# One weight difference from the DMA queue to VectorE, a quadrant fetched one step earlier, and a final norm by whole rows on VectorE

## The chip, the cores and the metric

The kernel runs on one core of a Trainium2 chip. A core has five engines with a queue each: TensorE (PE in the profile, with its weight loads as PEld), VectorE (DVE), ScalarE (ACT), GpSimd (POOL) and SyncE (SP). Each takes its own instructions in order and meets the others through semaphores. DMA transfers are issued from the queues of SP, ACT and POOL. The metric is device time in microseconds (us) of one execution; lower is better.

## The reference, cut to what matters

One layer of an encoder on 1024 positions of width 1024, in float32. The change touches the end of it, the down projection of the gated MLP and the last layer norm:

```python
def conv_ffn(x, w_up, conv_w, conv_b, w_down):
    h = depthwise_conv(x @ w_up, conv_w, conv_b)
    g, v = jnp.split(h, 2, axis=-1)
    return (jax.nn.silu(g) * v) @ w_down          # (1024 x 2816) @ (2816 x 1024)

h = layer_norm(DEEPNORM_ALPHA * h + ffn, ln_ffn_g[i], ln_ffn_b[i])
```

with `layer_norm(x) = (x - mean) * rsqrt(var + 1e-5) * g + b` over the 1024 columns of a row.

## The kernel before, in words

Every float32 product is made of three matmuls (`mm3`, L185, L187, L189): both operands are split into a rounded high part and the rest (`split`: a cast on ScalarE, L179, and a subtraction on VectorE, L176), and high times high, high times low and low times high are summed in PSUM.

The down projection is a block scheme of **seven products instead of eight**. The gated activations lie in DRAM (`gd`) as four quadrants `g(k, h)`, k the half of the inner dimension and h the half of the rows; the weights `wd` likewise as `w(k, h)`, h the half of the output columns. Product s = 0 to 6 multiplies a sum or difference of activation quadrants, `xa`, by one of weight quadrants, `xb`. Each product runs over six blocks b of the inner dimension (two slices of 128 each, the last one slice); a block is 24 matmuls in groups of three (12 in the last), so products 0 to 5 have 132 matmuls each. Product 6 runs row by row of the output, so that rows can be finished one after the other.

For every (s, b) three steps are recorded ahead of the matmuls: `down_load` fetches quadrants on SP's queue, `down_pile` adds to them, and `down_prep` splits `xa` into `ga` and `xb` into `wb`. Addition is done by the DMA itself: `pile` (L1095) is a DMA on POOL's queue that accumulates onto its destination. A subtraction is a `negate` on ScalarE (L1098), then a pile. Two tiles per block live long: `sst[b]` (named `sa`) is the running sum of activations, `tst[b]` (`sb`) that of weights. Product 3 needs xa = g(1,1) + sst and xb = tst - w(0,0); both start from a fresh fetch (`qa`, `qw`).

The order on PE, VectorE, ScalarE and POOL is the order in which the code records it (a manual schedule). At step n of the list of (s, b), `down_prep` is done up to two blocks ahead, `down_pile` and `down_load` some blocks more. `extra` adds the work between products: loading the residual (`acc`), adding a finished product's four PSUM banks to it (`down_out`, L1310), and residual scaling (L1178, L1179).

The end: after product 5, `last_row` takes rows 4 to 7 and then, as product 6 gives each, rows 0 to 3. It forms mean and variance (L1334, L217), the inverse deviation by a power on POOL (L218), and calls `finish`. There a row's first columns are done by two VectorE instructions and its last 512 (192 in row 3) by ScalarE and two POOL instructions (L1279, L1280); then SP sends the row out. Row 3, the last of all, goes out in three pieces.

Of the kernel before, what the change touches and what calls it, by code (L numbers as in the profile page):

```python
# [10 lines left out]
F32 = mybir.dt.float32  # L11
F32R = mybir.dt.float32r
AF = mybir.ActivationFunctionType
ALU = mybir.AluOpType
# [133 lines left out]
def encoder_layer(ctx: ExitStack, tc: tile.TileContext, a, out: bass.AP):  # L148
# [940 lines left out]
    def fetch(name, src, b):  # L1089
        t = t4([P, 2, 512], F32, name)  # L1090
        nc.sync.dma_start(out=t[:, 0 : span(b)], in_=src)
        return t
# [9 lines left out]
    def quads_of(b):  # L1102
# [5 lines left out]

        return g, w

    def down_load(s, b):
        g, w = quads_of(b)
        if s == 0:
            tst[b] = fetch(f"sb{b}", w(0, 0), b)
            dsrc[s, b] = fetch(f"qa{s}{b}", g(0, 0), b), tst[b]
        elif s == 1:
            sst[b] = fetch(f"sa{b}", g(0, 1), b)
            dsrc[s, b] = sst[b], tst[b]
        elif s == 2:
            dsrc[s, b] = sst[b], tst[b]  # L1120
        elif s == 3:
            dsrc[s, b] = fetch(f"qa{s}{b}", g(1, 1), b), fetch(f"qw{s}{b}", w(0, 0), b)
        elif s == 4:
            dsrc[s, b] = sst[b], fetch(f"qw{s}{b}", w(1, 1), b)
        elif s == 5:
            dsrc[s, b] = fetch(f"qa{s}{b}", g(1, 1), b), tst[b]
        else:
            dsrc[s, b] = fetch(f"qa{s}{b}", g(1, 0), b), fetch(f"qw{s}{b}", w(1, 0), b)

    def down_pile(s, b):  # L1130
        g, w = quads_of(b)
        n = span(b)
        xa, xb = dsrc[s, b]
        if s == 1:
            negate(xb, b)
            pile(xa, g(1, 1))
            pile(xb, w(0, 1))
        elif s == 2:
            negate(xa, b)
            negate(xb, b)  # L1140
            pile(xa, g(0, 0))
            pile(xb, w(1, 1))
        elif s == 3:
            negate(xb, b)
            pile(xa, sst[b][:, 0:n])
            pile(xb, tst[b][:, 0:n])
        elif s == 4:
            pile(xa, g(1, 0))
        elif s == 5:
            negate(xb, b)  # L1150
            pile(xb, w(1, 0))

    def down_prep(s, b):
        n = span(b)
        xa, xb = dsrc.pop((s, b))
        g = [t4([P, 2, 2, 256], F32R, f"ga{s}{b}{l}") for l in range(2)]
        w = [t4([P, 2, 512], F32R, f"wb{s}{b}{l}") for l in range(2)]
        split(g[0][:, 0:n], g[1][:, 0:n], xa[:, 0:n].rearrange("p k (j u) -> p k u j", u=2))
        hi, lo = [x[:, 0:n] for x in w]
        if s == 2:  # L1160
            nc.scalar.mul(hi, xb[:, 0:n], -1.0)
            nc.vector.scalar_tensor_tensor(
                out=lo, in0=xb[:, 0:n], scalar=-1.0, in1=raw(hi), op0=ALU.mult, op1=ALU.subtract
            )
        else:
            split(hi, lo, xb[:, 0:n])
        dops[s, b] = g, w
# [91 lines left out]
    def finish(i):  # L1259
        mv, rs = fin.pop(i)  # L1260
        rc = slice(i * P, (i + 1) * P)
        z = acc[i]
        n = 512 if i != 3 else 832
        c, d = slice(0, n), slice(n, 1024)
        nb = st([P, 1], F32, f"nb{i}")
        nc.vector.scalar_tensor_tensor(
            out=z[:, c], in0=z[:, c], scalar=mv[:, 0, 0:1], in1=ffg[:, c], op0=ALU.subtract, op1=ALU.mult
        )
        nc.vector.scalar_tensor_tensor(  # L1269
            out=nb, in0=mv[:, 0, 0:1], scalar=-1.0, in1=rs, op0=ALU.mult, op1=ALU.mult  # L1270
        )
        nc.scalar.activation(out=z[:, d], in_=z[:, d], func=AF.Identity, scale=rs, bias=nb)  # L1272
        for e in (c,) if i != 3 else (slice(0, 448), slice(448, n)):
            nc.vector.scalar_tensor_tensor(
                out=z[:, e], in0=z[:, e], scalar=rs, in1=ffb[:, e], op0=ALU.mult, op1=ALU.add
            )
            if i == 3:
                nc.sync.dma_start(out=out[rc, e], in_=z[:, e])
        nc.gpsimd.tensor_tensor(out=z[:, d], in0=z[:, d], in1=ffg[:, d], op=ALU.mult)  # L1279
        nc.gpsimd.tensor_tensor(out=z[:, d], in0=z[:, d], in1=ffb[:, d], op=ALU.add)  # L1280
        if i != 3:
            nc.sync.dma_start(out=out[rc], in_=z)
        else:
            nc.sync.dma_start(out=out[rc, d], in_=z[:, d])

    order = [(s, b) for s in range(7) for b in range(NB)]
    banks = {}
# [86 lines left out]
    for n, (s, b) in enumerate(order[: 6 * NB]):  # L1374
        if s < 2 and b == 0:
            banks[s] = [bank(f"dn{s}{rb}") for rb in range(4)]
        for step, lead in ((down_load, 3), (down_pile, 2), (down_prep, 0)):
            while done[step] < min(len(order), reach(n) + lead):
                step(*order[done[step]])
                done[step] += 1  # L1380
        down_mm(s, b, range(4), banks[s % 2], slice(0, 512), s < 2 and b == 0, b == NB - 1)
        extra(s, b)
        if (s, b) == (4, 0):
            ffg, ffb = row(5, "ffg"), row(6, "ffb")
# [36 lines left out]
```

## Time and profile before

| | |
|---|---|
| median of 3 runs | 880.27 us (879.35 to 881.75) |
| profiled execution | 879.64 us, of which the span from first to last instruction is 877.9 us |
| mean granted TensorE clock | 0.97 of full speed |
| TensorE busy | 813.2 us, 93% of the span |
| VectorE busy | 721.1 us, 82% |
| ScalarE, GpSimd busy | 401.8 us and 424.6 us |

The span is one profiled execution. Busy shares are means over stages with different limits, so a stage is read by itself: the rows below give stretches by their time from the start of the span. The down projection's products run from about 635 us on, the norm of the last rows from about 835 us. A row of the timeline gives the start, the duration, the engine, the line of the code, the operation and its tiles, and in brackets the idle time ahead of it with what ended it.

### The profile page before, as it was taken

The numbers are of one execution on the slowest core, as the hardware profiler recorded it, in microseconds if no ns is written. First come the engines' busy times: TensorE is split into PE (matmuls) and PEld (weight loads), VectorE is DVE, ScalarE is ACT, GpSimd is POOL, SyncE is SP. The second block draws the span as 40 slices with busy tenths as digits, with TensorE's granted clock in tenths as the row PEclk, the third lists the DMA queues.
The fourth block names the chain that finished last, engine by engine and source line by source line (L and its number), as shares of the span: only waits on it lengthen the run. The fifth ranks groups of instructions, "written<-read, shape, count | busy, mean of one in ns | idle before, by whom it ended". The sixth has DMA issues, their size and how long they took to land. (4 is left out here: it accounts for less than half of the span.)

```text
span 877.9 us, 10479 instructions
## 1 busy us (share of the span) xinstructions
PE 813.2 (93%) x3803; PEld 668.5 (76%) x3803; DVE 721.1 (82%) x980; ACT 401.8 (46%) x602; POOL 424.6 (48%) x274
## 2 busy tenths in 40 slices
PE   8984989967799999999999999999999999899992
PEld 6884967857688788888888888888878877688882
DVE  5999698999988898888888878888696865668856
ACT  4524381563354434444343444343564734466311
POOL 4579498878824455333455543334043322311075
PEclk9997999989899999999999999999999999999997
DMA  9305531131112223322222233222899999999212
GB/s 354 118 1 149 158 144 49 49 120 62 59 49 96 73 72 97 109 83 72 73 72 72 75 107 106 73 72 72 290 357 216 232 277 238 257 287 313 84 79 114
DMA packets 37492, 118.13 MB, mean 135 GB/s; under 512 B 4216, under 2 KB 5112, under 8 KB 37440
## 3 DMA queue, kind: packets, MB, share of 16 engines
q1 hardware_dynamic: 23408, 80.61, 26.2%
q0 software_dynamic: 7696, 25.31, 14.3%
q10 hardware_dynamic: 6336, 11.54, 3.5%
q8 instruction: 30, 0.49, 0.2%
q14 instruction: 22, 0.18, 0.1%
HBM read 91.75 MB, written 19.92 MB: 127 GB/s over the span
## 5 line engine op out<-in xcount | busy, mean ns | idle before, releaser
L1081 POOL TENSOR_TENSOR t<-t,t 128x1024 f32<-128x1024 f32 x22 | 54.6, 2482 | 241.3 <-DVE t L1046 177.1
L1046 DVE SCALAR_TENSOR_TENSOR t<-c,cols,t 128x1 f32<-128x1 f32 (+2 forms) x264 | 141.9, 585 | 3.7 <-ACT t L1071 0.5
L185 PE MATMUL by<-b,a 128*128 128x512 f32 (+1 forms) x268 | 106.2, 396 | 3.7 <-DVE c L922 3.7
L187 PE MATMUL dn<-wb,ga 128*128 128x512 f32 x264 | 105.2, 398 | 4.0 <-DVE wb L176 2.4
L185 PE MATMUL dn<-wb,ga 128*128 128x512 f32 x264 | 105.0, 398 | 3.7 <-DVE ga L176 2.3
L189 PE MATMUL by<-b,a 128*128 128x512 f32 (+1 forms) x268 | 105.6, 394 | 0.0
L187 PE MATMUL by<-b,a 128*128 128x512 f32 (+1 forms) x268 | 105.5, 394 | 0.0
L189 PE MATMUL dn<-wb,ga 128*128 128x512 f32 x264 | 104.5, 396 | 0.0
L176 DVE TENSOR_TENSOR a<-s,a 128x512 fp32r<-128x512 f32 x85 | 88.7, 1043 | 14.9 <-ACT a L873 14.6
L185 PE MATMUL bz<-b,a 128*128 128x512 f32 (+1 forms) x180 | 71.4, 397 | 3.5 <-DVE a L176 3.5
L187 PE MATMUL bz<-b,a 128*128 128x512 f32 (+1 forms) x180 | 71.3, 396 | 3.0 <-DVE b L176 3.0
L185 PE MATMUL bx<-b,a 128*128 128x512 f32 (+1 forms) x192 | 72.2, 376 | 1.2 <-ACT c L989 1.2
L176 DVE TENSOR_TENSOR a<-wr,a 128x512 fp32r<-128x512 f32 x64 | 71.5, 1120 | 1.9 <-ACT a L873 1.9
L187 PE MATMUL bx<-b,a 128*128 128x512 f32 (+1 forms) x192 | 71.9, 375 | 0.0
L189 PE MATMUL bx<-b,a 128*128 128x512 f32 (+1 forms) x192 | 71.9, 374 | 0.0
L189 PE MATMUL bz<-b,a 128*128 128x512 f32 (+1 forms) x180 | 71.1, 395 | 0.0
L185 PEld LDWEIGHTS by<-b,a 128*128 128x128 f32 x268 | 51.3, 191 | 16.1 <-DVE c L922 4.9
L187 PEld LDWEIGHTS dn<-wb,ga 128*128 128x128 f32 x264 | 49.9, 189 | 17.8 <-DVE wb L176 4.2
L185 PEld LDWEIGHTS dn<-wb,ga 128*128 128x128 f32 x264 | 50.0, 189 | 16.3 <-ACT wb L179 2.7
L922 DVE TENSOR_TENSOR c<-bz,c 128x512 f32<-128x512 f32 x44 | 30.4, 691 | 38.8 <-PE bz L189 38.0
L1230 ACT COPY c<-bx 128x512 f32<-128x512 f32 x22 | 12.9, 587 | 104.7 <-DVE c L922 104.7
L189 PEld LDWEIGHTS by<-b,a 128*128 128x128 f32 x268 | 51.2, 191 | 11.6
(340 smaller groups left out, 2005.5 us busy)
## 6 DMA issues: line engine op xcount, KB each, us to landing
wr<-wup SPq DMA_DIRECT2D x44, 512.0 KB, 4.5
gd<-t ACTq DMA_DIRECT2D x44, 256.0 KB
qa<-gd SPq DMA_DIRECT2D x20, 512.0 KB, 6.0
sa<-gd POOLq DMA_DIRECT2D x15, 512.0 KB, 15.7
sb<-wd POOLq DMA_DIRECT2D x15, 512.0 KB, 12.2
qw<-wd SPq DMA_DIRECT2D x15, 512.0 KB, 10.1
winT<-winT SPq DMA_DIRECT2D x8, 512.0 KB, 7.3
x<-x SPq DMA_DIRECT2D x8, 512.0 KB, 10.7
```

What stands on the lines that cost most here:

```text
L176: eng.tensor_tensor(out=lo, in0=src, in1=raw(hi), op=ALU.subtract)
L185: nc.tensor.matmul(outs[i], ll, rh[i], start=first, stop=False, **kw)
L187: nc.tensor.matmul(outs[i], lh, rl[i], start=False, stop=False, **kw)
L189: nc.tensor.matmul(outs[i], lh, rh[i], start=False, stop=last, **kw)
L922: nc.vector.tensor_tensor(out=o, in0=b, in1=x, op=ALU.add)
L1046: nc.vector.scalar_tensor_tensor(out=t[:, lo:hi], in0=c[:, lo + sh : hi + sh], scalar=w[:, wi : wi + 1], in1=t[:, lo:hi], op0=ALU.mult, op ...
L1081: nc.gpsimd.tensor_tensor(out=tg, in0=tg, in1=tv, op=ALU.mult)
L1230: nc.scalar.copy(out=cg[:, 0:512], in_=bx[j])
```

## The change

Three edits. In product 3 the weight difference is no longer a `negate` on ScalarE and an accumulating DMA, but one subtraction on VectorE at the head of `down_prep`. The fetch of `sst[b]` is recorded in product 0 (`early`) instead of in product 1's `down_load`. In `finish` a row is two VectorE instructions over all 1024 columns; only row 3 gives 224 columns of its second step to ScalarE and POOL, and ACT's queue sends that piece.

```diff
+    def early(b):
+        sst[b] = fetch(f"sa{b}", quads_of(b)[0](0, 1), b)
+
     def down_load(s, b):
...
         elif s == 1:
-            sst[b] = fetch(f"sa{b}", g(0, 1), b)
             dsrc[s, b] = sst[b], tst[b]
...
         elif s == 3:
-            negate(xb, b)
             pile(xa, sst[b][:, 0:n])
-            pile(xb, tst[b][:, 0:n])
...
     def down_prep(s, b):
         n = span(b)
         xa, xb = dsrc.pop((s, b))
+        if s == 3:
+            nc.vector.tensor_tensor(out=xb[:, 0:n], in0=tst[b][:, 0:n], in1=xb[:, 0:n], op=ALU.subtract)
...
         z = acc[i]
-        n = 512 if i != 3 else 832
-        c, d = slice(0, n), slice(n, 1024)
-        nb = st([P, 1], F32, f"nb{i}")
         nc.vector.scalar_tensor_tensor(
-            out=z[:, c], in0=z[:, c], scalar=mv[:, 0, 0:1], in1=ffg[:, c], op0=ALU.subtract, op1=ALU.mult
+            out=z, in0=z, scalar=mv[:, 0, 0:1], in1=ffg, op0=ALU.subtract, op1=ALU.mult
         )
-        nc.vector.scalar_tensor_tensor(
-            out=nb, in0=mv[:, 0, 0:1], scalar=-1.0, in1=rs, op0=ALU.mult, op1=ALU.mult
-        )
-        nc.scalar.activation(out=z[:, d], in_=z[:, d], func=AF.Identity, scale=rs, bias=nb)
-        for e in (c,) if i != 3 else (slice(0, 448), slice(448, n)):
+        pieces = (slice(0, 1024),) if i != 3 else (slice(0, 400), slice(400, 800))
+        if i == 3:
+            d = slice(800, 1024)
+            nc.scalar.activation(out=z[:, d], in_=z[:, d], func=AF.Identity, scale=rs)
+            nc.gpsimd.tensor_tensor(out=z[:, d], in0=z[:, d], in1=ffb[:, d], op=ALU.add)
+        for e in pieces:
             nc.vector.scalar_tensor_tensor(
                 out=z[:, e], in0=z[:, e], scalar=rs, in1=ffb[:, e], op0=ALU.mult, op1=ALU.add
             )
...
-        nc.gpsimd.tensor_tensor(out=z[:, d], in0=z[:, d], in1=ffg[:, d], op=ALU.mult)
-        nc.gpsimd.tensor_tensor(out=z[:, d], in0=z[:, d], in1=ffb[:, d], op=ALU.add)
...
+            nc.sync.dma_start(out=out[rc, e], in_=z[:, e])
+        if i == 3:
+            nc.scalar.dma_start(out=out[rc, d], in_=z[:, d])
...
+        if s == 0:
+            early(b)
         down_mm(s, b, range(4), banks[s % 2], slice(0, 512), s < 2 and b == 0, b == NB - 1)
```

POOL's queue, from product 3's piles on (`qa` is xa, `qw` is xb), before:

```order
L1095 DMA qa_5752<-sa_5290 128x1024
L1095 DMA qw_5754<-sb_4985 128x1024
L1095 DMA qa_5794<-sa_5334 128x1024
L1095 DMA qw_5796<-sb_5110 128x1024
L1095 DMA qa_5835<-sa_5375 128x1024
L1095 DMA qw_5837<-sb_5114 128x1024
```

and now, with the first pile of product 4 (`sa<-gd`) as the last row:

```order
L1095 DMA qa_5752<-sa_5248 128x1024
L1095 DMA qa_5794<-sa_5300 128x1024
L1095 DMA qa_5833<-sa_5347 128x1024
L1095 DMA qa_5872<-sa_5388 128x1024
L1095 DMA qa_5912<-sa_5427 128x1024
L1095 DMA qa_5938<-sa_5466 128x512
L1095 DMA sa_5248<-gd 128x1024
```

The six weight piles are gone from this queue, and the six activation piles follow each other without a step of ScalarE between them.

VectorE, the preparation of product 3's blocks 3 to 5, right behind the eight additions of product 2's banks, before:

```order
L176 TENSOR_TENSOR ga_5997<-qa_5876,ga_5996 128x1024
L176 TENSOR_TENSOR wb_5999<-qw_5878,wb_5998 128x1024
L176 TENSOR_TENSOR ga_6032<-qa_5917,ga_6031 128x1024
L176 TENSOR_TENSOR wb_6034<-qw_5919,wb_6033 128x1024
L176 TENSOR_TENSOR ga_6067<-qa_5944,ga_6066 128x512
L176 TENSOR_TENSOR wb_6069<-qw_5946,wb_6068 128x512
```

and now:

```order
L1157 TENSOR_TENSOR qw_5874<-sb_5228,qw_5874 128x1024
L176 TENSOR_TENSOR ga_5989<-qa_5872,ga_5988 128x1024
L176 TENSOR_TENSOR wb_5991<-qw_5874,wb_5990 128x1024
L1157 TENSOR_TENSOR qw_5914<-sb_5232,qw_5914 128x1024
L176 TENSOR_TENSOR ga_6025<-qa_5912,ga_6024 128x1024
L176 TENSOR_TENSOR wb_6027<-qw_5914,wb_6026 128x1024
L1157 TENSOR_TENSOR qw_5940<-sb_5236,qw_5940 128x512
L176 TENSOR_TENSOR ga_6061<-qa_5938,ga_6060 128x512
L176 TENSOR_TENSOR wb_6063<-qw_5940,wb_6062 128x512
```

Each block has a third VectorE instruction, which stands ahead of the block's two splits.

VectorE at the end, row 4 and the begin of row 5, before:

```order
L1334 BN_AGGR omv_6636<-obs_6500 128x2
L217 TENSOR_SCALAR o4v<-omv_6636 128x1
L1266 SCALAR_TENSOR_TENSOR acc_5326<-acc_5326,omv_6636,ffg 128x512
L1269 SCALAR_TENSOR_TENSOR nb_6642<-omv_6636,o4rs 128x1
L1274 SCALAR_TENSOR_TENSOR acc_5326<-acc_5326,o4rs,ffb 128x512
L1334 BN_AGGR omv_6650<-obs_6502 128x2
```

and now:

```order
L1329 BN_AGGR omv_6630<-obs_6494 128x2
L217 TENSOR_SCALAR o4v<-omv_6630 128x1
L1265 SCALAR_TENSOR_TENSOR acc_5328<-acc_5328,omv_6630,ffg 128x1024
L1274 SCALAR_TENSOR_TENSOR acc_5328<-acc_5328,o4rs,ffb 128x1024
L1329 BN_AGGR omv_6639<-obs_6496 128x2
```

The small instruction for ScalarE's bias is gone and both row instructions are twice as wide; on POOL only the power (L218) is left of each of the rows 4 to 7 and 0 to 2.

## Rows read from the trace of the kernel before

**Rows 1.** The page: busy time by engine.

```profile
PE 813.2 (93%) x3803; PEld 668.5 (76%) x3803; DVE 721.1 (82%) x980; ACT 401.8 (46%) x602; POOL 424.6 (48%) x274
```

**Rows 2.** Busy time in stretches: length, PE, PEld, DVE, ACT, POOL, clock, DMA, GB/s.

```profile
730.00:745.00 15.00, 15.00 (x66) 11.78 (x65) 6.62 (x7) 5.30 (x5) 3.12 (x4) 1.00 1.06 246
...
748.00:752.00 4.00, 2.80 (x8) 2.05 (x9) 4.00 (x7) 0.59 (x2) 0.87 (x1) 0.79 1.05 262
```

**Rows 3.** Waits of the weight loads, 600 to 878: us in total, times, longest.

```profile
PEld dn L187 <- DVE wb L176: 4.2, 5, 2.2
PEld dn L185 <- ACT wb L179: 2.7, 1, 2.7
PEld dn L185 <- ACT wb L1161: 2.2, 2, 1.2
PEld dn L187 <- DVE wb L1162: 2.1, 2, 1.1
```

**Rows 4.** Timeline of PE: first matmul of product 3, first of product 6, a later one.

```profile
734.74 0.40 PE L185 MATMUL dn<-wb,ga 128*128 128x512 f32 x1
...
831.56 0.40 PE L185 MATMUL dl<-wb,ga 128*128 128x512 f32 x1
...
842.66 0.39 PE L185 MATMUL dl<-wb,ga 128*128 128x512 f32 x1
```

**Rows 5.** Timeline of ACT in product 3.

```profile
730.20 1.11 ACT L179 CAST ga<-qa 128x1024 fp32r<-128x1024 f32 x1 [0.88 <-DMA qa<-sa]
...
745.16 1.06 ACT L1098 ACTIVATE qw<-qw 128x1024 f32<-128x1024 f32 x1 [5.75 <-DMA qw<-wd]
```

**Rows 6.** Timeline of POOL: first pile of product 1, first weight pile of product 3.

```profile
654.59 0.93 POOL L1095 DMA_DIRECT2D sa<-gd  x1
...
718.86 0.87 POOL L1095 DMA_DIRECT2D qw<-sb  x1 [5.36 <-ACT qw L1098]
```

**Rows 7.** DMA queues, 690 to 770: packets, MB, share of 16 engines.

```profile
q0 software_dynamic: 3734, 12.55, 79.4%
```

**Rows 8.** Negations of product 3's weights: ns min/median/max, first and last start.

```profile
L1098 ACT ACTIVATE qw<-qw x6: 632/1044/1059, 717.5 to 751.6; 128x1024 f32<-128x1024 f32 x5, 128x512 f32<-128x512 f32 x1
```

**Rows 9.** Timeline of DVE in product 3: a split, and the eight bank additions.

```profile
731.35 1.23 DVE L176 TENSOR_TENSOR ga<-qa,ga 128x1024 fp32r<-128x1024 f32 x1 [0.92 <-ACT ga L179]
...
749.53 4.87 DVE L1310 TENSOR_TENSOR acc<-acc,dn 128x512 f32<-128x512 f32 x8
```

**Rows 10.** Timeline of DVE at the end: rows 4, 5, 0 and 3 of the output.

```profile
835.24 0.74 DVE L1266 SCALAR_TENSOR_TENSOR acc<-acc,omv,ffg 128x512 f32<-128x512 f32 x1
836.44 0.16 DVE L1269 SCALAR_TENSOR_TENSOR nb<-omv,o4rs 128x1 f32<-128x1 f32 x1 [0.46 <-POOL o4rs L218]
...
837.49 0.74 DVE L1266 SCALAR_TENSOR_TENSOR acc<-acc,omv,ffg 128x512 f32<-128x512 f32 x1
...
851.73 0.68 DVE L1398 TENSOR_TENSOR acc<-acc,dl 128x512 f32<-128x512 f32 x1
...
853.49 1.80 DVE L1266 SCALAR_TENSOR_TENSOR acc<-acc,omv,ffg 128x512 f32<-128x512 f32 x1
...
865.92 0.41 DVE L1398 TENSOR_TENSOR acc<-acc,dl 128x256 f32<-128x256 f32 x1
...
867.95 1.80 DVE L1266 SCALAR_TENSOR_TENSOR acc<-acc,omv,ffg 128x832 f32<-128x832 f32 x1
```

**Rows 11.** Timeline of POOL at the end: the powers of rows 4 and 5.

```profile
835.41 1.00 POOL L218 TENSOR_TENSOR o4rs<-o4v,small 128x1 f32<-128x1 f32 x1 [35.70 <-DVE o4v L217]
...
840.70 0.55 POOL L218 TENSOR_TENSOR o5rs<-o5v,small 128x1 f32<-128x1 f32 x1
```

**Rows 12.** Timeline of PEld and ACT: last weight load, ScalarE's piece of row 3.

```profile
861.98 0.19 PEld L189 LDWEIGHTS dl<-wb,ga 128*128 128x128 f32 x1
...
870.39 0.55 ACT L1272 ACTIVATE acc<-acc,nb,o3rs 128x192 f32<-128x192 f32 x1 [4.20 <-DVE nb L1269]
```

**Rows 13.** Timeline of SP: the last transfer's issue.

```profile
872.62 0.33 SPq L1284 DMA_DIRECT2D out<-acc  x1
```

More of the change, by code (lines that the diff above doesn't have):

```diff
@@ L1276, in finish @@
             )
-            if i == 3:
-                nc.sync.dma_start(out=out[rc, e], in_=z[:, e])
-        nc.gpsimd.tensor_tensor(out=z[:, d], in0=z[:, d], in1=ffg[:, d], op=ALU.mult)
-        nc.gpsimd.tensor_tensor(out=z[:, d], in0=z[:, d], in1=ffb[:, d], op=ALU.add)
[L1281 to L1284, printed above, removed]
+            nc.sync.dma_start(out=out[rc, e], in_=z[:, e])
+        if i == 3:
+            nc.scalar.dma_start(out=out[rc, d], in_=z[:, d])
     order = [(s, b) for s in range(7) for b in range(NB)]
```

## The prediction

> **What bounds the kernel now.** I read the page first: TensorE is busy 93% of the span [rows 1], so a gain must come out of the remaining 7% or out of the tail behind the last product. Next the stretches: inside product 3 the DMA engines are busy without a gap (share 1.06) while VectorE works 6.62 of 15 us [rows 2]. POOL's software queue, which carries the accumulating piles, takes 79.4% of sixteen engines over 80 us for 12.55 MB [rows 7]. So the middle of the down projection is short of DMA, not of VectorE. Then the waits of the weight loads, which show where TensorE stops in the down projection [rows 3], and the timelines at these waits and at the end.
>
> *Product 3.* The matmul pitch: between the first matmul of product 6 at 831.56 and a later one at 842.66 there are 48, so 11.10 / 48 = 0.2313 us [rows 4]; 132 of them take 30.5 us. Products 4 and 5 (264 matmuls, 61.05 us) end where product 6 starts, so product 4 started at about 770.5. Product 3 started at 734.74 [rows 4] and so took 35.8 us, **5.3 us** more than its matmuls need. The longest waits sit there: 2.7 us for one weight cast and part of the 4.2 us for the weight split [rows 3]; the clock granted in 748 to 752 falls to a mean of 0.79 [rows 2], between the levels of 1.2 and 2.4 GHz, right behind the long wait. The cause shows on ScalarE: at 745.16 it has been idle 5.75 us in front of a negation whose `qw` has not landed from DRAM [rows 5]. ScalarE takes its queue in order, so the casts of block 2, needed at 734.74 + 2 x 5.55 = 745.8, stand behind it. POOL's queue in turn waits for the negation: 5.36 us ahead of a weight pile [rows 6]. The loop is DMA, ScalarE, DMA, ScalarE, VectorE, TensorE.
>
> *The tail.* The last weight load is at 861.98 [rows 12], the last row's first addition on VectorE only at 865.92 [rows 10]: VectorE comes 3.5 us late. It is late because each row goes through POOL: the powers of rows 4 and 5 are 5.3 us apart [rows 11] as POOL also has two instructions per row behind ScalarE's piece, and VectorE waits for the power.
>
> **The change part by part.**
>
> *The weight difference.* Gone are six negations, 1.04 us each for five of them [rows 8], and six piles: five of 512 KB and one of 256 KB. From [rows 7], 12.55 MB in 0.794 x 80 = 63.5 us is 5.06 us a MB; the six are 2.88 MB, so about 14.6 us of all sixteen engines go. Added are six VectorE subtractions; the nearest row is the split with the same operands, 1.23 us for 1024 columns [rows 9]; with a 512-column one at 0.68 [rows 10] that is 6.8 us. They must hide beside the matmuls, and the tightest place is block 3, behind the eight bank additions (4.87 us, [rows 9]). Laid end to end from block 0's split at 731.35: two further instructions for block 0 (2.46), two residual ones (1.37, at 0.68 each as the additions of that size), three for blocks 1 and 2 each (7.38), the additions (4.87), block 3's three (3.69): 751.1. TensorE needs block 3 at 734.74 + 3 x 5.55 = 751.4. So the cover just holds, by 0.3 us; blocks 4 and 5 have 5.55 us each for 3.69 us of work. Activation piles: the first is behind the product before, so the cast at 730.20 stays where it is [rows 5]; the others now follow without a step of ScalarE, 0.52 x 5.06 = 2.7 us each, so they land at about 2.7 us intervals against a need every 5.55 us. Nothing is left that is late in product 3: all of the 5.3 us goes. Bounds: 5.3 (all) and 0 (the fetch itself, not the loop, is late).
>
> What is late next lies in product 2: 2.2 us of waits for L1161 and 2.1 us for L1162 [rows 3]. Those operands come through piles queued ahead of the removed ones, so I leave them as they are; the bound is −4.3.
>
> *`early`.* It moves fetches of 512 KB past loads of the residual on SP's queue. The first pile on `sa`, at 654.59, issued without a wait [rows 6], so the fetch was not late: worth 0. If the residual loads are late instead, they have a whole product of slack.
>
> *The final norm.* A 512-column row instruction takes 0.74 us [rows 10]. An addition takes 0.68 for 512 columns and 0.41 for 256 [rows 10], 0.27 per 256, so 1024 columns take 0.74 + 0.54 = **1.28 us**. Row 4 to row 5 was 837.49 − 835.24 = 2.25 us on VectorE with the power wait of 0.46 in it [rows 10]; both row instructions widen by 0.54 and the small one goes (0.07 net): 3.3 us. Four rows from 835.24 end at 848.3. Rows 0 to 2 have addition and statistics ahead of the first instruction (853.49 − 851.73 = 1.76), then 1.28 + 0.46 + 1.28: 4.78 each, 862.6 in all. That is within 0.3 us of where TensorE ends, some 0.4 after the load at 861.98 [rows 12]. The last row's addition so comes at 862.7 instead of 865.92. From it to the first row instruction 867.95 − 865.92 = 2.03 [rows 10]; then 1.28, the power 0.46, and the longer of two paths: VectorE's two pieces of 400 columns (0.6 each), or ScalarE's 224 columns (0.55 for 192, [rows 12]) and one POOL addition. From that ScalarE start at 870.39 to the last issue at 872.62 [rows 12, 13] lie 2.23 us with two POOL steps; less ScalarE's 0.55 that is 0.84 per step. So 862.7 + 2.03 + 1.28 + 0.46 + 0.1 + 0.6 + 0.8 = 867.9, against 872.62: **−4.7 to −4.8**. In the same clock of before, bounds are −5.8 (no power wait in the chain) and what rival D gives. Part of it is that row 3's first instruction was stretched to 1.80 us while POOL worked on the row before [rows 10], where 832 columns should take 0.74 + 0.34 = 1.08; that POOL work goes.
>
> The Trainium skill, page "SBUF — State Buffer", section "Who interferes with whom", says that a VectorE instruction with two SBUF inputs contends with a GpSimd instruction that reads SBUF, and for the whole instruction. The stretched 1.80 us rows agree.
>
> *Sum.* −5.3 − 4.8 = −10.1 on an execution of 879.64 us: 869.5. That execution lies 0.6 under the median of 880.27, so **870.2 us** beside the median.
>
> **The rivals.**
>
> *A: product 3 still waits.* The fetches of `qa` and `qw` share DMA engines that are full [rows 2]; if the fetch, not the loop, is the limit, only the tail's 4.8 comes: 875.5. For it: the idle 5.75 us ended on a fetch [rows 5]. Against it: 14.6 us of DMA work goes just ahead of these fetches.
>
> *B: VectorE becomes the bound in product 3.* The margin of block 3 is 0.3 us by rows laid end to end. If none of the subtractions is hidden, 6.8 us come where 5.3 went: 870.2 + 6.8 = 877.0. Against it: VectorE idle 8.4 of 15 us [rows 2]. The Trainium skill, page "Perfetto Trace Analysis", section "Optimizing Scalar/DVE Operations", speaks for this rival: it advises to take work from VectorE to ScalarE or GpSimd where VectorE is saturated, and this change goes the other way at 82% over the span. The stretch's own row does not show saturation.
>
> *C: product 2's waits go too.* With less DMA ahead its piles may land sooner; 4.1 of the 4.3 us: 866.1. For it: the queue is one, and it is full. Against it: the removed piles stand behind those of product 2, and the first of them at 718.86 [rows 6].
>
> *D, the other side: stretched row instructions.* If the whole-row instructions are stretched as the 1.80 us rows are, each takes t in place of 1.28, and about sixteen of them stand in the chain of the tail: the change is −10.1 + 16 (t − 1.28), zero at t = 1.91. At 1.80 + 0.54 = 2.34 it is +6.9: 887. For it: the row at 853.49, 1.80 us for 512 columns [rows 10]. Against it: what stretched that one was POOL at work beside it, and the change leaves POOL only the powers and one addition. The power shows it from the other side: 1.00 us beside VectorE's row instruction, 0.55 alone [rows 11]. By the rule cited above, D would need POOL reads throughout the tail.
>
> **How the numbers follow.** Forecast 0.62 (869 to 872), A 0.15 (875.5), B 0.06 (877), C 0.12 (866), D 0.03 (from 880 up), no change at all 0.02. The likeliest gives 870.2. The range goes down to C (865.5) and up to A with a margin (876): it leaves out D, no change and most of B. Measurement tells about 0.3%, 2.6 us. Forecast, A, B and C are all faster by more: 0.95; same 0.02; slower 0.03.
>
> **What would show it.** In the profile after: no negations of `qw` and no piles `qw<-sb`; six subtractions of some 1.2 us; no wait of weight loads for splits or casts within product 3, no fall of the clock there, and product 3 at about 30.5 us. Product 2's waits still there. In the tail the last weight load at about 861.98 − 5.3 = 856.7, the last row's first addition within 1 us of TensorE's end, row instructions at 1.28 us, the last issue about 10 us sooner. Wrong it would be if block 3 of product 3 waits for VectorE (B), if ScalarE's casts still wait for `qa` or VectorE's subtraction for the fetch of `qw` (A), or if the row instructions take nearer 1.9 us (D).

## The result, and the profile after

The changed kernel takes **869.57 us** (median of 6 runs, 866.98 to 871.30) beside 880.7 us for the kernel before: ratio 0.9871, 95% interval 0.985 to 0.9892, or 11.4 us by the ratio. Run once more on another occasion it took 866.95 us, a ratio of 0.9842 (0.9819 to 0.9865), or 13.9 us. The forecast was 870.2 us, a ratio of 0.9886. The profiled execution is the fastest of the first six, 866.98 us with a span of 865.2 us; it lies 2.6 us under the median, which matters below.

The page, busy time by engine, answers to [rows 1]. VectorE gained 11 us of work, POOL and ScalarE lost 20 and 11:

```profile
PE 810.0 (94%) x3803; PEld 667.0 (77%) x3803; DVE 732.2 (85%) x978; ACT 390.9 (45%) x589; POOL 404.1 (47%) x253
```

The first matmuls of products 2, 3, 4 and 6, from the timeline of PE after, as in [rows 4]:

```profile
701.30 0.39 PE L185 MATMUL dn<-wb,ga 128*128 128x512 f32 x1
...
733.39 0.39 PE L185 MATMUL dn<-wb,ga 128*128 128x512 f32 x1
...
764.07 0.40 PE L185 MATMUL dn<-wb,ga 128*128 128x512 f32 x1
...
825.13 0.39 PE L185 MATMUL dl<-wb,ga 128*128 128x512 f32 x1
```

The first matmuls of products 2 and 4 before, beside [rows 4]:

```profile
700.23 0.40 PE L185 MATMUL dn<-wb,ga 128*128 128x512 f32 x1
...
770.56 0.39 PE L185 MATMUL dn<-wb,ga 128*128 128x512 f32 x1
```

Product 3 takes 764.07 − 733.39 = 30.68 us (770.56 − 734.74 = 35.82 before), product 2 32.09 us (34.51 before), and from the start of product 6 to the end of the span it is 865.2 − 825.13 = 40.07 us (877.9 − 831.56 = 46.34 before). This last stretch is called the tail from here on. These three differences, −5.1, −2.4 and −6.3, less 1.1 us by which product 0 starts later in this execution, are the 12.7 us between the spans. The waits of the weight loads after, 600 to 878 (beside [rows 3]), show no cast of product 3:

```profile
PEld dn L187 <- DVE wb L176: 3.2, 4, 2.2
PEld dn L187 <- DVE wb L1164: 1.1, 1, 1.1
PEld dn L185 <- ACT wb L1163: 0.6, 1, 0.6
```

Of the first line 2.7 us, the 2.2 us among them, lie in product 0 and are there in both kernels; the other two waits, 0.24 and 0.26 us, are in product 3. L1163 and L1164 are product 2. Product 3 as a stretch, and the place of the clock dip of [rows 2] (length, PE, PEld, DVE, ACT, POOL, clock, DMA, GB/s):

```profile
733.39:764.07 30.68, 30.68 (x134) 24.63 (x133) 30.01 (x34) 17.50 (x18) 7.11 (x8) 1.00 1.06 280
748.00:752.00 4.00, 4.00 (x18) 3.10 (x17) 3.96 (x4) 2.57 (x3) 1.48 (x2) 1.00 1.04 256
```

TensorE is busy throughout and the clock stays at its upper level, 2.4 GHz. VectorE is busy 30.01 of 30.68 us, but from 756.17 on it already prepares product 4, so the cover is read from its timeline: block 0's first split, and block 3 right behind the bank additions.

```profile
731.04 1.22 DVE L176 TENSOR_TENSOR ga<-qa,ga 128x1024 fp32r<-128x1024 f32 x1
...
746.64 1.22 DVE L1157 TENSOR_TENSOR qw<-sb,qw 128x1024 f32<-128x1024 f32 x1
747.78 1.22 DVE L176 TENSOR_TENSOR ga<-qa,ga 128x1024 fp32r<-128x1024 f32 x1
749.04 1.23 DVE L176 TENSOR_TENSOR wb<-qw,wb 128x1024 fp32r<-128x1024 f32 x1
```

Block 3 ends at 750.27; TensorE wants it at 733.39 + 3 x 5.55 = 750.04. The margin forecast was 0.3 us; it was −0.2 us, and TensorE's weight load waits 0.26 us for it. The other wait, 0.24 us, is for block 0.

The tail, on DVE (rows 4, 5 and 3 of the output, to be held against [rows 10]):

```profile
828.81 1.27 DVE L1265 SCALAR_TENSOR_TENSOR acc<-acc,omv,ffg 128x1024 f32<-128x1024 f32 x1
830.54 1.29 DVE L1274 SCALAR_TENSOR_TENSOR acc<-acc,o4rs,ffb 128x1024 f32<-128x1024 f32 x1 [0.46 <-POOL o4rs L218]
...
832.05 1.27 DVE L1265 SCALAR_TENSOR_TENSOR acc<-acc,omv,ffg 128x1024 f32<-128x1024 f32 x1
...
855.46 0.42 DVE L1395 TENSOR_TENSOR acc<-acc,dl 128x256 f32<-128x256 f32 x1
...
856.25 0.40 DVE L1395 TENSOR_TENSOR acc<-acc,dl 128x256 f32<-128x256 f32 x1
...
857.49 1.27 DVE L1265 SCALAR_TENSOR_TENSOR acc<-acc,omv,ffg 128x1024 f32<-128x1024 f32 x1
```

A whole-row instruction takes 1.27 to 1.29 us (forecast 1.28), and from row 4 to row 5 it is 3.24 us (forecast 3.3). The last weight load and the last issues after, from the timelines of PEld, SP and ACT (beside [rows 12, 13]):

```profile
855.62 0.19 PEld L189 LDWEIGHTS dl<-wb,ga 128*128 128x128 f32 x1
...
859.87 1.34 SPq L1277 DMA_DIRECT2D out<-acc  x2
...
860.45 1.26 ACTq L1279 DMA_DIRECT2D out<-acc  x1
```

(SP's row is two issues in one.) VectorE meets TensorE at its end: the first half of the last row's piece is added at 855.46, the second at 856.25, 0.6 us behind the last load.

### The profile page after: what moved, and what is told of

Its sections match the earlier page's. It is cut to its first block, busy times and chain, and to the rows that moved or that the text cites. A ratio compares the mean times of both kernels' runs of the same rounds, so it can differ in the third digit from the quotient of the medians.

```text
span 865.2 us, 10439 instructions
## 1 busy us (share of the span) xinstructions
PE 810.0 (94%) x3803; PEld 667.0 (77%) x3803; DVE 732.2 (85%) x978; ACT 390.9 (45%) x589; POOL 404.1 (47%) x253
## 4 chain that ended last, share of the span: by engine, by line
PE 54%; DVE 8%; issue 5%; DMA 4%; POOL 4%; ACT 1%; DVEq 0%; SPq 0%; ACTq 0%; POOLq 0%
PE by L185 6%; PE by L189 6%; PE by L187 6%; PE bz L185 4%; PE bz L187 4%; PE bz L189 4%; PE bx L185 4%; PE bx L189 4%; PE bx L187 4%; PE dn L187 4%; PE dn L189 4%; PE dn L185 4%; DMA sb<-wd 2%; DVE a L176 2%; DVE t L1046 1%
## 5 line engine op out<-in xcount | busy, mean ns | idle before, releaser
L185 PE MATMUL by<-b,a 128*128 128x512 f32 (+1 forms) x268 | 105.2, 392 | 3.4 <-DVE c L922 2.8
L189 PE MATMUL by<-b,a 128*128 128x512 f32 (+1 forms) x268 | 104.5, 390 | 0.0
L187 PE MATMUL by<-b,a 128*128 128x512 f32 (+1 forms) x268 | 104.4, 389 | 0.0
L185 PEld LDWEIGHTS by<-b,a 128*128 128x128 f32 x268 | 50.4, 188 | 16.0 <-DVE c L922 3.7
L187 PEld LDWEIGHTS dn<-wb,ga 128*128 128x128 f32 x264 | 49.6, 188 | 15.6 <-DVE wb L176 3.2
L189 PEld LDWEIGHTS by<-b,a 128*128 128x128 f32 x268 | 50.3, 188 | 11.5
L187 PEld LDWEIGHTS by<-b,a 128*128 128x128 f32 x268 | 50.4, 188 | 11.0
## 6 DMA issues: line engine op xcount, KB each, us to landing
sb<-wd POOLq DMA_DIRECT2D x15, 512.0 KB, 11.6
```

What stands on the lines that cost most here:

```text
L185: nc.tensor.matmul(outs[i], ll, rh[i], start=first, stop=False, **kw)
L187: nc.tensor.matmul(outs[i], lh, rl[i], start=False, stop=False, **kw)
L189: nc.tensor.matmul(outs[i], lh, rh[i], start=False, stop=last, **kw)
```

## The experiments

The lengths in this table are worked out as above, from the first matmuls of each product and the span of the run's profile; the ratio is to the kernel before, on the same chip in the same stretch of time. A length comes from one execution: product 3 of the same code took 35.8, 34.4 and 37.5 us in the first, fifth and sixth line, so the verdicts go by the ratios.

| kernel | product 2 | product 3 | tail | ratio (95% interval) |
|---|---|---|---|---|
| before | 34.5 | 35.8 | 46.3 | 1 |
| changed | 32.1 | 30.7 | 40.1 | 0.9871 (0.985 to 0.9892) |
| changed, again | 34.8 | 30.6 | 40.0 | 0.9842 (0.9819 to 0.9865) |
| weight difference alone | 35.4 | 30.6 | 45.8 | 0.9931 (0.9915 to 0.9948) |
| norm alone | 35.7 | 34.4 | 40.6 | 0.9938 (0.9923 to 0.9953) |
| earlier fetch alone | 32.2 | 37.5 | 46.4 | 0.9993 (0.998 to 1.0006) |
| piles back, no negation | 35.7 | 33.8 | 40.6 | 0.9933 (0.9915 to 0.9951) |
| negation back, no piles | 34.9 | 30.6 | 40.1 | 0.9885 (0.9869 to 0.9901) |
| idle piles added | 35.9 | 33.2 | 40.5 | 0.9956 (0.9943 to 0.997) |
| product 2 likewise | 33.0 | 30.6 | 39.6 | 0.9884 (0.987 to 0.9897) |
| idle work on POOL | 35.3 | 30.6 | 47.2 | 0.9969 (0.9957 to 0.9981) |
| both sums, three blocks early | 35.4 | 31.3 | 39.8 | 0.9889 (0.987 to 0.9908) |
| both sums, all blocks | 33.4 | 31.6 | 39.6 | 0.9883 (0.9866 to 0.9901) |
| product 2, four blocks | 33.3 | 30.5 | 39.8 | 0.9859 (0.9837 to 0.988) |

### The three edits one by one

The diff ahead of the prediction, cut in three, each put on the kernel before. The weight difference alone:

```diff
-            negate(xb, b)
             pile(xa, sst[b][:, 0:n])
-            pile(xb, tst[b][:, 0:n])
...
+        if s == 3:
+            nc.vector.tensor_tensor(out=xb[:, 0:n], in0=tst[b][:, 0:n], in1=xb[:, 0:n], op=ALU.subtract)
```

> The weight difference on VectorE alone, without the earlier fetch and without the new norm. Between the two profiles product 3 went from 35.8 to 30.7 us and product 2 from 34.5 to 32.1 us. Theory P (both come from the removed negations and piles): 5 to 7.5 us faster than before, product 3 at 30.7 us, product 2 at about 32 us. Rival theory Q (product 2's gain is the earlier fetch of the activation sums): 5 us faster, product 2 still at 34.5 us. The tail from the start of product 6 on stays at 46.3 us by either.

Measured: 6.1 us faster (0.69% of 879.73; interval 4.6 to 7.5). Product 3 at 30.6 us; product 2 did not gain, at 35.4 us.

The norm alone (the whole edit of `finish`; two of its lines):

```diff
-        n = 512 if i != 3 else 832
+        pieces = (slice(0, 1024),) if i != 3 else (slice(0, 400), slice(400, 800))
```

> The final norm by whole rows alone. Theory P: the tail from the start of product 6 to the end of the span falls from 46.3 to about 40.1 us, nothing ahead of it changes: 4.8 (forecast) to 6.3 us (read off the profile after) faster than before. Rival (the tail gained because the stages ahead of it left POOL's and the DMA queues in another state): the tail alone gains under 4 us.

Measured: 5.5 us faster (interval 4.1 to 6.8), the tail at 40.6 us. Both terms of the sum stand by themselves, and 6.1 + 5.5 = 11.6 us is what the whole change gave at first (11.4, 9.5 to 13.2); the second time it gave a little more (13.9, 11.9 to 15.9).

The earlier fetch alone (without the lines that define `early` and take the fetch out of `down_load`):

```diff
...
+        if s == 0:
+            early(b)
```

> The earlier fetch of the activation sums alone. Theory P: no difference within 0.3%, products 0 to 3 as long as before. Theory Q: product 2 is 2.4 us shorter than its 34.5 us and the kernel 2 to 2.5 us faster.

Measured: nothing, 0.9993 with 1 inside the interval. This profile is of use for another reason: product 2 is short here, 32.2 us, and product 3 takes it back at 37.5 us. Behind a longer stop there, the granted clock over 7 us is 0.53, that is the lower level of 1.2 GHz for most of the stretch (same columns as above):

```profile
747.90:755.00 7.10, 6.46 (x15) 4.92 (x16) 7.10 (x11) 2.63 (x3) 4.04 (x6) 0.53 1.07 271
```

### Was it ScalarE's queue or the piles?

The change took away the negations and the piles together. The edits from here on are put on the changed kernel. First the piles back without the negations. Since the pile makes `xb` the sum of fetched quadrant and running sum, twice the running sum less that is the same difference:

```diff
             pile(xa, sst[b][:, 0:n])
+            pile(xb, tst[b][:, 0:n])
...
-            nc.vector.tensor_tensor(out=xb[:, 0:n], in0=tst[b][:, 0:n], in1=xb[:, 0:n], op=ALU.subtract)
+            nc.vector.scalar_tensor_tensor(
+                out=xb[:, 0:n], in0=tst[b][:, 0:n], scalar=2.0, in1=xb[:, 0:n], op0=ALU.mult, op1=ALU.subtract
+            )
```

> The changed kernel, but with the six weight piles of product 3 put back onto the fetched quadrant (so it becomes the sum of the fetched quadrant and the running sum) and VectorE takes it from twice the running sum, which gives the same difference. The 2.88 MB of DMA traffic is back, ScalarE's negations are not. Theory L (the loss in product 3 was ScalarE's queue: casts behind a negation that waits for a fetch): product 3 stays near 31 us, and only product 2 may go back to 34.5 us: 0 to 2.5 us slower than the changed kernel. Theory T (the loss was the piles' DMA traffic): product 3 goes back to about 35 us: 4 to 7 us slower than the changed kernel.

Measured: 874.15 us, 0.9933, which is what the norm alone gives (0.9938). ScalarE is free of product 3's negations and nothing is gained by it: product 3 is at 33.8 us. In this kernel VectorE waits in ScalarE's place, so the run rules out ScalarE's queue but does not yet tell the load of the piles from a chain that is one transfer longer; the third run does. VectorE's timeline shows the subtraction of block 2 waiting for its pile; that of block 3 starts at 752.50, behind the bank additions:

```profile
744.18 1.23 DVE L1158 SCALAR_TENSOR_TENSOR qw<-sb,qw 128x1024 f32<-128x1024 f32 x1 [3.34 <-DMA qw<-sb]
```

The other way round, ScalarE's negations at their old place and no piles:

```diff
+            negate(xb, b)
             pile(xa, sst[b][:, 0:n])
...
-            nc.vector.tensor_tensor(out=xb[:, 0:n], in0=tst[b][:, 0:n], in1=xb[:, 0:n], op=ALU.subtract)
+            nc.vector.tensor_tensor(out=xb[:, 0:n], in0=tst[b][:, 0:n], in1=xb[:, 0:n], op=ALU.add)
```

> The changed kernel with ScalarE's six negations back at their old place in ScalarE's queue, but no weight piles: VectorE adds the running sum to the negated quadrant. Theory L (ScalarE's queue made the loss in product 3): casts stand again behind a negation that waits for its fetch, product 3 back at 33 to 36 us, 3 to 5 us slower than the changed kernel. Theory T (the piles' DMA work made it: a fetch or a pile lands late because the DMA engines are full): the fetches now land early enough, product 3 stays at about 30.7 us, within 1 us of the changed kernel.

Measured: 869.81 us, 0.9885; product 3 at 30.6 us. The negations cost nothing there. Timeline of ACT:

```profile
739.70 1.06 ACT L1098 ACTIVATE qw<-qw 128x1024 f32<-128x1024 f32 x1 [2.60 <-DMA qw<-wd]
740.67 1.09 ACT L179 CAST ga<-qa 128x1024 fp32r<-128x1024 f32 x1
741.67 1.05 ACT L179 CAST wb<-qw 128x1024 fp32r<-128x1024 f32 x1
```

The same two casts stand behind a waiting negation as in [rows 5], but counted from the start of product 3 that negation begins 6.5 us sooner (739.70 − 735.79 against 745.16 − 734.74), its fetch having landed sooner, and the casts are in time. The fetch itself, a plain one on SP's queue, was issued 1.7 us ahead of product 3 and landed 12.1 us later before (733.02 to 745.16); here it was issued 3.1 us ahead and landed 7.1 us later (732.65 to 739.70).

Third, the changed kernel with six accumulating DMAs added that nothing waits for and that go to an unused place in DRAM:

```diff
             pile(xa, sst[b][:, 0:n])
+            nc.gpsimd.dma_start(out=idle[b, :, 0:n], in_=tst[b][:, 0:n], accum_op=ALU.add)
```

> The changed kernel with six accumulating DMAs added that nothing waits for: in product 3, behind each activation pile, the running weight sum of the block is accumulated onto an unused place in DRAM, 2.88 MB, as many bytes as the removed piles moved. Theory T (traffic itself): the waits of products 2 and 3 come back though no engine waits for these DMAs, 3 to 5 us slower than the changed kernel. Rival theory S (what cost time in the run with the piles put back was the latency of fetch plus pile in the chain to one block's cast, not the load on the DMA engines): no more than 1 us slower.

Measured: 876.31 us, 0.9956: 6.7 us slower than the changed kernel by the medians, and no faster than the norm alone (0.9938), in which all the piles are at work. All that the edit in product 3 gave is gone: 2.5 us of it in product 3 itself (33.2 us), 2.6 in product 4 (33.1 us, 30.5 in the changed kernel) and the rest in product 2 and the tail. The DMA view of 690 to 770, with the queue (packets, MB, share of 16 engines) and the landing of the added DMAs (count, KB, median us):

```profile
q0 software_dynamic: 3695, 12.42, 78.6%
...
idle<-sb POOLq DMA_DIRECT2D x5, 512.0 KB, 21.2
```

The timeline of ACT in the same kernel, where casts wait for the activation piles:

```profile
742.80 1.11 ACT L179 CAST ga<-qa 128x1024 fp32r<-128x1024 f32 x1 [4.52 <-DMA qa<-sa]
749.51 1.12 ACT L179 CAST ga<-qa 128x1024 fp32r<-128x1024 f32 x1 [4.64 <-DMA qa<-sa]
756.82 1.11 ACT L179 CAST ga<-qa 128x1024 fp32r<-128x1024 f32 x1 [3.44 <-DMA qa<-sa]
```

With two accumulating DMAs a block the activations come 6.7 and 7.3 us apart, where TensorE takes 5.55 us a block. So it is the load of the piles that delays, and that even where no engine waits for them. (The added DMAs hold POOL's queue for 4.1 us in all, as two of them wait for the sum that they read; the pile behind each of the two waited 3.26 and 1.75 us longer for other things.) For the changed kernel the queue's row in the same window, under [rows 7]:

```profile
q0 software_dynamic: 3348, 11.13, 70.6%
```

How fast the queue is can be read in product 2 of the changed kernel, where each block still needs two piles. The piles of the three rows below were issued 16 to 20 us earlier (at 697.25, 702.28 and 703.22), so the queue was not waiting for work. Timeline of ACT, a cast behind each pile:

```profile
715.20 1.06 ACT L1163 ACTIVATE wb<-sb 128x1024 fp32r<-128x1024 f32 x1 [2.69 <-DMA sb<-wd]
...
719.00 1.12 ACT L179 CAST ga<-sa 128x1024 fp32r<-128x1024 f32 x1 [2.73 <-DMA sa<-gd]
...
722.81 1.06 ACT L1163 ACTIVATE wb<-sb 128x1024 fp32r<-128x1024 f32 x1 [2.70 <-DMA sb<-wd]
```

They come 3.8 us apart: two piles a block make 7.6 us and one makes 3.8 us, on either side of TensorE's 5.55 us.

### The tail's other side

Idle work on POOL behind each power (its result is not used):

```diff
+        if i != 3:
+            t = t4([P, 512], F32, f"idle{i}")
+            nc.gpsimd.tensor_tensor(out=t, in0=ffg[:, 0:512], in1=ffb[:, 0:512], op=ALU.add)
```

> The changed kernel with one idle addition of 512 columns on POOL behind the power of rows 4 to 7 and 0 to 2; nothing uses its result. If a VectorE row instruction is stretched whenever POOL reads beside it (what rival D needs), the second row instruction takes 1.8 to 2.5 us in place of 1.28, seven of them in the chain: 4 to 8 us slower than the changed kernel less what TensorE's end hides (none, VectorE sets the chain). If the stretched rows of before had another cause: within 1 us.

Measured: 877.78 us, 0.9969, the tail at 47.2 us. Timelines of DVE and POOL, row 4:

```profile
832.50 1.27 DVE L1265 SCALAR_TENSOR_TENSOR acc<-acc,omv,ffg 128x1024 f32<-128x1024 f32 x1
834.24 2.31 DVE L1274 SCALAR_TENSOR_TENSOR acc<-acc,o4rs,ffb 128x1024 f32<-128x1024 f32 x1 [0.46 <-POOL o4rs L218]
```

```profile
832.68 1.53 POOL L218 TENSOR_TENSOR o4rs<-o4v,small 128x1 f32<-128x1 f32 x1 [46.03 <-DVE o4v L217]
834.18 1.28 POOL L1280 TENSOR_TENSOR idle<-ffg,ffb 128x512 f32<-128x512 f32 x1
```

The row instruction that starts beside POOL's takes 2.27 to 2.31 us in place of 1.28 in the seven rows: 7 x 1.03 = 7.2 us, and the tail grew by 47.17 − 40.07 = 7.1. Rival D's price is real, and only the absence of POOL work in the tail keeps it away. The power shows the same from the other side: it is in flight beside VectorE's first instruction for 1.53 us, 0.55 alone [rows 11].

### The changed kernel again, and more of the same

> The changed kernel once more, without an edit. In nine profiles product 2 is either about 32.1 us or 34.5 to 35.9 us long, also in kernels that are alike up to there. Theory V (product 2's shorter time in the profile after was that execution's luck and not the change): the median is again about 870 us, and the profile shows product 2 at 32 or at 35 us, product 3 at 30.6 us, the tail at 40.1 us. If the change shortens product 2 for good, this profile shows it at 32 us again.

Measured without an edit: 866.95 us, 0.9842. Product 2 is at 34.8 us here. Of the gains in the first profile after, the 2.4 us of product 2 are therefore not shown to be the change's: it is 32 to 36 us long with or without it.

Three kernels carry the exchange of piles for VectorE further. All of product 2's weights:

```diff
-            dsrc[s, b] = sst[b], tst[b]
+            dsrc[s, b] = sst[b], fetch(f"qw{s}{b}", w(1, 1), b)
...
-            negate(xb, b)
-            pile(xb, w(1, 1))
...
+        if s == 2:
+            nc.vector.tensor_tensor(out=tst[b][:, 0:n], in0=xb[:, 0:n], in1=tst[b][:, 0:n], op=ALU.subtract)
+            xb = tst[b]
```

> The changed kernel with the same exchange one product earlier: product 2's weights are fetched plainly and VectorE subtracts the running sum from them, in place of a negation on ScalarE and a pile; 2.88 MB of accumulating DMA becomes plain fetches. Theory T: product 2's remaining 1.7 us of waits go, product 2 at 30.6 us in place of 32.1 (up to 35.7 in other profiles): 1.5 to 4 us faster than the changed kernel. Rival: the fetches take buffers that the later products' fetches then lack, product 2 or 3 waits for these: same or slower.

Measured: 869.96 us, 0.9884, no gain. Product 1 now takes 33.6 us (30.6 before): the wait has moved there. That the six fetches run beside product 1's piles is the likely reason, but was not tried by itself. The same for blocks 2 to 5 only:

```diff
+            if b < 2:
+                negate(xb, b)
...
+        if s == 2 and b >= 2:
```

> The changed kernel with product 2's weights of blocks 2 to 5 alone fetched plainly and subtracted on VectorE; blocks 0 and 1 keep negation and pile. In every profile the casts of product 2 come 3.8 us apart, one pile each, so two piles a block take 7.6 us where TensorE needs 5.55 us a block. Theory T (the rate of the accumulating queue): from block 2 on one pile a block is left, 3.8 us, product 2 falls to about 31 us (34.8 and 32.1 us in the two profiles of the changed kernel), without the load on product 1 that the run with all six blocks had: ratio to the kernel before 0.980 to 0.984, where the changed kernel had 0.987 and 0.984. Rival (the plain fetches take bandwidth from the piles that remain and the waits only move, as in the run with all six): ratio 0.985 to 0.990.

Measured: 867.79 us, 0.9859, between the two values of the changed kernel: no difference that can be told. Product 1 stays at 30.8 us, but product 2 is still at 33.3 us, so the theory's expectation failed and the rival's ratio came.

Both sums of product 3 on VectorE, for blocks 0 to 2, recorded early:

```diff
+    def both3(b, xa, xb, both):
+        n = span(b)
+        nc.vector.tensor_tensor(out=xb[:, 0:n], in0=tst[b][:, 0:n], in1=xb[:, 0:n], op=ALU.subtract)
+        if both:
+            nc.vector.tensor_tensor(out=xa[:, 0:n], in0=xa[:, 0:n], in1=sst[b][:, 0:n], op=ALU.add)
...
+        elif s == 3 and b < 3:
+            both3(b, xa, xb, True)
...
-        if s == 3:
-            nc.vector.tensor_tensor(out=xb[:, 0:n], in0=tst[b][:, 0:n], in1=xb[:, 0:n], op=ALU.subtract)
+        if s == 3 and b >= 3:
+            both3(b, xa, xb, False)
```

> The changed kernel, and for blocks 0 to 2 of product 3 both sums on VectorE (the difference of the weights and the sum of the activations, three further piles less), recorded where the piles were recorded, that is in product 2, where VectorE is idle some 9 us of 34. Theory T: 1.5 MB less of accumulating DMA while product 2 waits for its last piles; product 2 falls from 32 to 35 us to about 31 us, product 3 stays at 30.6 us: 2 to 4 us faster than the changed kernel. Rival: VectorE, which takes its queue in order, now waits in product 2 for the fetches of product 3 and holds up product 2's splits: same or slower.

Measured: 870.74 us, 3.8 us slower than the changed kernel measured beside it (866.95 us); the two profiled spans differ by 1.4 us only (867.7 and 866.3). Timeline of DVE: two sums stand ahead of the first splits of product 3, which begins at 735.61, and the second split ends too late for it (a wait of 0.89 us; product 3 is 0.7 us longer).

```profile
731.85 1.22 DVE L1134 TENSOR_TENSOR qw<-sb,qw 128x1024 f32<-128x1024 f32 x1
732.98 1.22 DVE L1136 TENSOR_TENSOR qa<-qa,sa 128x1024 f32<-128x1024 f32 x1
734.12 1.22 DVE L176 TENSOR_TENSOR ga<-qa,ga 128x1024 fp32r<-128x1024 f32 x1
735.25 1.22 DVE L176 TENSOR_TENSOR wb<-qw,wb 128x1024 fp32r<-128x1024 f32 x1
```

For all blocks (the step of blocks 0 to 2 as above, and no pile left in product 3):

```diff
+        if s == 3 and b >= 3:
+            both3(b, xa, xb, True)
```

> As the run with three blocks, and blocks 3 to 5 have the sum of the activations on VectorE as well, at the head of their preparation; product 3 has no pile at all. Theory T alone: as fast as the run with three blocks or faster. Rival B of the prediction (VectorE becomes the bound): block 3 has no margin in the profile after, so up to three more instructions of 1.14 us behind the bank additions delay it: product 3 at 31 to 34 us, 0 to 3.4 us slower than the run with three blocks.

Measured: 870.01 us, 3.1 us slower than the changed kernel measured beside it (0.9 us by the profiled spans). The share of the software queue in 690 to 770 is down to this, and still product 2 has 33.4 us:

```profile
q0 software_dynamic: 2450, 8.11, 53.6%
```

So product 3's piles are not what makes product 2 wait, and VectorE has no room for more in product 3: it is at 31.6 us, with waits of 0.88 and 0.35 us for VectorE's splits. No version beat the changed kernel.

## Why the prediction was right, and where not

**The number.** 870.2 us forecast, 869.57 and 866.95 us measured; faster, as forecast. By the ratios the saving was 11.4 and 13.9 us where 10.1 was forecast; the tail gave more than its term. That product 3's size came out was luck as far as its cause goes: the edit removes the negations and the piles together, so it gives the same size whichever of them is to blame.

**Product 3: the size held, the cause did not.** −5.3 us forecast, −5.1 us in the profile, 6.1 us (4.6 to 7.5) for the edit alone, half a us of it at the very end of the span (see the tail). But the step "The loop is DMA, ScalarE, DMA, ScalarE, VectorE, TensorE", with ScalarE's queue as the cause, fell: with the negations in and the piles out all of the gain is there, with the piles in and the negations out it is not, and piles that nobody waits for bring the loss back. The row in front of the negation, idle 5.75 us, named the fetch as the releaser, and that was the thing to follow. What misled is the price of a pile: 0.52 x 5.06 = 2.7 us each from the queue's share, by which two piles a block (5.3 us) just keep up with TensorE (5.55 us). That price leaves out that the DMA engines also carry the plain fetches and are never free in that stretch (share 1.06, [rows 2]). By the clock the same row gives more: 12.55 MB in 80 us are 24 piles of 0.52 MB, so 3.3 us each (an estimate from [rows 7]), 6.7 us for two. Measured they are 3.8 us apart in product 2, and a pair takes 6.7 to 7.3 us with the idle piles. Two piles a block are too many for TensorE's 5.55 us; one is not. Whether the load acts through the order of the software queue or through the sixteen engines that both queues share was not separated; that a plain fetch on SP's queue took 7.1 us in place of 12.1 speaks for a part of the second.

**VectorE's cover** was right to 0.5 us, 0.3 forecast and −0.2 measured. The sum leaves out that block 0's own subtraction now stands ahead of its first split: this split begins 2.35 us ahead of product 3 (731.04) where it began 3.39 us ahead before; in return the chain from there to the end of block 3 is 19.2 us and not 19.8. It is the limit: rival B did not come about, but the two kernels that put activation sums on VectorE as well were 3 to 4 us slower than the changed one beside them, about 1 us of it seen as waits for VectorE in product 3. The advice of the Trainium skill, page "Perfetto Trace Analysis", section "Optimizing Scalar/DVE Operations", that offloading may make sense where VectorE is saturated, speaks against those two and not against the change; the runs agree.

**`early`**: forecast at nothing, measured 0.9993.

**The tail**: −4.8 us forecast (the terms as written add up to 867.97, which is −4.65), −5.5 us (4.1 to 6.8) for the edit alone, −6.3 us in the profile. The mechanism and the single rows were right; the term was mis-sized at two places. First, the last row's first addition comes 855.46 − 825.13 = 30.33 us after the start of product 6, before 865.92 − 831.56 = 34.36: −4.0 us, not −3.2. A row of 0 to 2 takes 4.68 us (850.78 less 846.10 on VectorE's timeline) and not 4.78, a row of 4 to 7 3.24 and not 3.3, and behind row 7 the sum counts the statistics of a next row that is not there (2.92 us, 841.42 less 838.50). Second, the sum ends at the last issue and takes the rest of the span as unchanged. POOL's last instruction, before and after:

```profile
872.01 0.59 POOL L1280 TENSOR_TENSOR acc<-acc,ffb 128x192 f32<-128x192 f32 x1
```

```profile
859.77 0.66 POOL L1272 TENSOR_TENSOR acc<-acc,ffb 128x224 f32<-128x224 f32 x1 [0.59 <-ACT acc L1271]
```

From the addition to the end of this instruction it is 6.68 us before and 4.97 after (−1.7). From there to the end of the span it is 877.9 − 872.60 = 5.30 us before and 865.2 − 860.43 = 4.77 after, −0.5 us for which the prediction has no term. This half us is not the norm's but comes with the six piles: the stretch is 5.2 to 5.3 us in all five profiles with the old number of DMAs on POOL's queue, the norm alone among them, and 4.7 to 4.8 us in all five with six fewer, the weight difference alone among them (its tail is 45.8 us with the old norm).

**Rival A** did not occur, but its premise, that full DMA engines make the fetch late, is what the experiments bear out; the change removed that load, as the argument against A said. **Rival C**, product 2's waits going as well, seemed to happen in the profile; the second profile and the three edits one by one show that product 2's length varies by itself. **Rival D** needs POOL at work in the tail; a row instruction then takes 2.31 us, where the prediction reckoned with 2.34.

## What to carry to other kernels

When an engine idles in front of a step that itself waits for a transfer, price the transfer queue at its measured spacing per transfer, against the consumer's time per block, before blaming the engine's order: a share of busy time, on engines that another queue uses too, hid here that two transfers a block were too many and one was not. An exchange of traffic for engine time pays only up to the engine's own margin in that stage, so lay its instructions end to end between the two points that matter; the second helping of the same exchange gained nothing. One profile can hold 2 us that are not the change's: repeat it before explaining them.

## What the runs showed of the hardware

- A VectorE row instruction with two inputs in SBUF, started beside a POOL addition of 1.28 us, takes 2.31 us in place of 1.28: it waits for nearly the whole of the other. The Trainium skill, page "SBUF — State Buffer", section "Who interferes with whom", says that a VectorE instruction with two SBUF inputs contends with a GpSimd instruction that reads SBUF, and calls the shared pair of ports an exclusive lock; the trace agrees (1.03 us of 1.28 lost).
- Accumulating DMAs of 512 KB came 3.8 us apart in product 2 of the changed kernel. The landing of one from the running sum took 16.8 us in 730 to 746 before and 8.5 us after, as the DMA views of the two traces show (count, KB, median us):

```profile
qa<-sa POOLq DMA_DIRECT2D x2, 512.0 KB, 16.8
```

```profile
qa<-sa POOLq DMA_DIRECT2D x1, 512.0 KB, 8.5
```

- The end of the span comes later the more DMAs POOL's queue has issued in the whole run. From the end of POOL's last instruction to the end of the span it is 5.23 to 5.30 us with 54 of them (five profiles), 4.74 to 4.79 with 48 (five), 4.53 with 45, 4.44 with 44 and 4.30 with 42 (two): about 0.08 us for each. It is read across kernels that differ in other things too, and why it is so no run shows.
- A stop of TensorE costs more than its length at times. In the weight-difference run a pair of stops in product 2 (1.25 and 1.08 us of waiting weight loads, from 719.6 on) left a granted clock of 0.76 over the stretch around it; in the changed kernel's second profile two such pairs (1.10 and 1.07 us, 1.19 and 1.07 us) left it at 1.00. What decides between the two no run here tells.

```profile
718.00:725.00 7.00, 5.43 (x16) 3.81 (x15) 4.86 (x5) 2.17 (x2) 0.87 (x1) 0.76 1.05 279
```

```profile
716.00:727.00 11.00, 8.06 (x32) 5.49 (x31) 6.69 (x7) 3.90 (x4) 1.74 (x2) 1.00 1.07 266
```
